# Interleaving two float32 tensors: the first x tile loaded as four half-height pieces from two DMA rings

## The chip, the cores and the metric

The kernel runs on one core of a Trainium2 chip. The metric is the device time in microseconds of one execution, of which the runs shown give the median. A span is what the profiler recorded of one execution, from the program's first instruction to its last.

## The reference

Two tensors of 32 x 256 x 1024 float32 are woven into one of twice the width: elements of x on the even places of the last dimension, elements of y on the odd ones. Nothing is calculated.

```python
batch, seq, dim = x.shape                 # 32, 256, 1024
result = np.zeros((batch, seq, dim * 2), dtype=np.float32)
result[..., 0::2] = x
result[..., 1::2] = y
```

x and y are 33.55 MB each and the result is 67.11 MB, so 134.22 MB pass between HBM and SBUF.

## The kernel before

Because weaving doesn't depend on where a row ends, the kernel treats each tensor as one flat run of numbers. It cuts x and y into n = 8 tiles of 128 partitions by W = 8192 numbers (4 MB each), and the result into 8 tiles of 128 by 2W. One partition's share of a tile is 32 KB, contiguous in HBM. There are two buffers for x (`xt`), two for y (`yt`) and two for the output (`ot`); an output buffer holds one half (h = 0 or 1) of an output tile, 128 x 8192 numbers or 4 MB, made from H = 4096 columns of x and the same columns of y.

Three engines do the work, each with a loop of its own over the tiles, and they meet only through semaphores:

- SyncE issues all loads on its own DMA ring. The first x tile is loaded in two column halves (L42, which counts on `xsem[0]`, and L43, which counts on `hsem`). Then follow, tile by tile, x (L50) and y (L53), each as one transfer. From the third tile on it first waits (`woven`, counted by the copies) until the copies have read the old contents of the buffer.
- VectorE makes two copies per half tile: x to the even places of `ot[h]` (L67) and y to the odd ones (L70). Ahead of the copy of x it waits for the x tile, and for the stores of that output buffer to be over (`osem`, and for the second tile `qsem`).
- ScalarE issues all stores on its own ring, one per half tile (L83), after the second copy of that half. The very first half tile's store is made in two parts: the first quarter of the columns (L77) and the rest (L81).

A DMA adds 16 to its semaphore when it is complete, which is why waits are for multiples of 16. At the end ScalarE clears the semaphores and SyncE waits for the last store (L91).

The program begins with a barrier of all engines (in the traces under L99 and L137, the lines of the call). `tile_interleave_kernel` moves transfers ahead of it after the program is built: for each entry in the list of L104 it takes that engine's first remaining DMA from the later blocks, requires that it has no wait, and inserts it into the first block ahead of that engine's drain, with which the engine enters the barrier. Before the change the list has SyncE twice, so the two halves of the first x tile (L42, L43) are issued ahead of the barrier. The y tile of L53 is then SyncE's first transfer behind it.

Of the kernel before, what the change touches and what calls it, by code (L numbers as in the profile page):

```python
# [3 lines left out]


def _interleave(nc, x, y, out):
    P = 128
    W = 8192
    H = W // 2  # L10

    total = 1
    for s in x.shape:
        total *= s
    n = total // (P * W)
    assert n * P * W == total

    def rows(ap, names, k):
        flat = ap.rearrange("b s d -> (b s d)")
        return flat[k * names : (k + 1) * names].rearrange("(p w) -> p w", p=P)  # L20

    fp32 = mybir.dt.float32
    xt = [nc.alloc_sbuf_tensor(f"xt{b}", [P, W], fp32).ap() for b in (0, 1)]
    yt = [nc.alloc_sbuf_tensor(f"yt{b}", [P, W], fp32).ap() for b in (0, 1)]
    ot = [nc.alloc_sbuf_tensor(f"ot{b}", [P, W], fp32).ap() for b in (0, 1)]

    xsem = [nc.alloc_semaphore(f"xsem{b}") for b in (0, 1)]
    hsem = nc.alloc_semaphore("hsem")
    qsem = nc.alloc_semaphore("qsem")
    ysem = [nc.alloc_semaphore(f"ysem{b}") for b in (0, 1)]  # L30
    woven = nc.alloc_semaphore("woven")
    osem = [nc.alloc_semaphore(f"osem{b}") for b in (0, 1)]


    cuts = [0, W // 4, W]
    parts = [slice(a, b) for a, b in zip(cuts, cuts[1:])]

    xs = [rows(x, P * W, k) for k in range(n)]
    ys = [rows(y, P * W, k) for k in range(n)]
    os_ = [rows(out, 2 * P * W, k) for k in range(n)]  # L40

    nc.sync.dma_start(out=xt[0][:, :H], in_=xs[0][:, :H]).then_inc(xsem[0], 16)  # L42
    nc.sync.dma_start(out=xt[0][:, H:], in_=xs[0][:, H:]).then_inc(hsem, 16)  # L43

    for k in range(n):
        b = k % 2
        if k >= 2:
            nc.sync.wait_ge(woven, 4 * (k - 2) + 3)
        if k:
            nc.sync.dma_start(out=xt[b], in_=xs[k]).then_inc(xsem[b], 16)  # L50
        if k >= 2:
            nc.sync.wait_ge(woven, 4 * (k - 2) + 4)
        nc.sync.dma_start(out=yt[b], in_=ys[k]).then_inc(ysem[b], 16)  # L53

    for k in range(n):
        b = k % 2
        for h in (0, 1):
            c = slice(h * H, (h + 1) * H)
            if h == 0:
                nc.vector.wait_ge(xsem[b], 16 * (k // 2 + 1))  # L60
            elif k == 0:
                nc.vector.wait_ge(hsem, 16)
            if k:
                nc.vector.wait_ge(osem[h], 16 * k)
            if (k, h) == (1, 0):
                nc.vector.wait_ge(qsem, 16)
            nc.vector.tensor_copy(out=ot[h][:, 0::2], in_=xt[b][:, c]).then_inc(woven, 1)  # L67
            if h == 0:
                nc.vector.wait_ge(ysem[b], 16 * (k // 2 + 1))
            nc.vector.tensor_copy(out=ot[h][:, 1::2], in_=yt[b][:, c]).then_inc(woven, 1)  # L70

    for k in range(n):
        for h in (0, 1):
            nc.scalar.wait_ge(woven, 4 * k + 2 * h + 2)
            if (k, h) == (0, 0):
                for c in parts[:-1]:
                    nc.scalar.dma_start(  # L77
                        out=os_[k][:, c], in_=ot[h][:, c]
                    ).then_inc(qsem, 16)
                c = parts[-1]  # L80
                nc.scalar.dma_start(out=os_[k][:, c], in_=ot[h][:, c]).then_inc(osem[h], 16)  # L81
                continue
            nc.scalar.dma_start(  # L83
                out=os_[k][:, h * W : (h + 1) * W], in_=ot[h]
            ).then_inc(osem[h], 16)

    nc.scalar.wait_ge(osem[0], 16 * n)
    used = sorted(s.num for s in [*xsem, hsem, qsem, *ysem, woven, osem[0]])
    assert used == list(range(used[0], used[-1] + 1)), used
    nc.scalar.sem_clear(range(used[0], used[-1] + 1))  # L90
    nc.sync.nop(nofuse=True).wait_op(osem[1], 16 * n, "sem-ge").then_inc(  # L91
        osem[1], -16 * n
    )


def kernel(tc, x, y, out):
    nc = tc.nc
    tc.close()
    tc.compile()  # L99

    _interleave(nc, x, y, out)

    blocks = nc.main_func.blocks
    for engine in (mybir.EngineType.SP, mybir.EngineType.SP):  # L104
        opening = blocks[0].instructions
        at, moved = next(
            (b, i)
            for b in blocks[1:]
            for i in b.instructions
            if i.engine == engine and i.opcode == "DMACopy"  # L110
        )
        assert not (moved.sync_info and moved.sync_info.on_wait)
        body = at.instructions
        body.remove(moved)
        gate = next(
            n
            for n, i in enumerate(opening)
            if i.engine == engine and i.opcode == "Drain"
        )
        opening.insert(gate, moved)  # L120
        at.instructions = body
        blocks[0].instructions = opening


# [1 line left out]
_INS = ['x', 'y']  # L126
_OUTS = [((32, 256, 2048), 'float32')]


# [23 lines left out]
```

## Time and profile before

| What | Value |
|---|---|
| Time, median of 3 runs | 314.18 us (314.18 to 314.37) |
| Span of the profiled execution | 312.9 us, 114 instructions (the page gives no other time of it) |
| VectorE | 72.0 us busy, 23%, 32 copies: L67 36.7 us, 2295 ns each; L70 36.6 us, 2288 ns each |
| GpSimd | 0.2 us, four memsets of the opening |
| TensorE, ScalarE | no busy time (ScalarE only issues DMAs) |
| DMA | 134.22 MB in 4896 packets, mean 429 GB/s |
| Idle time ahead of L67 | 213.8 us, of it 206.5 until stores are over, 7.3 until the first x is there |
| Idle time ahead of L70 | 12.3 us, once, until the first y is there |
| From issue to landing | store of 4 MB 34.1 us; y 41.5; x 24.3; first x halves 7.3 and 11.8 (medians) |

Idle time of an engine that isn't the bottleneck costs nothing. VectorE's 213.8 us are of this kind if the transfers run on during it. The time from issue to landing has the waiting behind earlier transfers in it, and is far above what a transfer's own bytes take.

### The profile page before, as it was taken

What the parts mean: (1) busy time and instruction counts of PE and PEld (TensorE: products, weight loads), DVE (VectorE), ACT (ScalarE), POOL (GpSimd) and SP (SyncE); (2) the same over time, 40 slices, a digit from 0 to 9 for tenths busy, and PEclk for the clock granted to TensorE, in tenths of its full rate; (3) what the DMA queues carried; (4) which work ended last, traced back from release to release, by engine and by line L of the source; (5) the groups of instructions that cost most, each with busy time, mean ns of one, the idle gap of its engine ahead of it and who ended that gap; (6) DMA issues with size and microseconds to landing.
All of it is one profiled execution on the core that took longest, in us unless ns stands there. A gap on an engine that the chain in (4) does not pass through costs nothing.

```text
span 312.9 us, 114 instructions
## 1 busy us (share of the span) xinstructions
DVE 72.0 (23%) x32; POOL 0.2 (0%) x4
## 2 busy tenths in 40 slices
DVE  0216000501305023050220503205032050415410
POOL 0000000000000000000000000000000000000000
DMA  8999999999999999999999999999999999999998
GB/s 337 467 402 436 436 402 419 452 457 415 427 444 411 461 402 469 402 469 402 469 402 465 406 440 432 423 448 402 469 402 469 402 469 402 469 402 448 423 423 381
DMA packets 4896, 134.22 MB, mean 429 GB/s; under 512 B 544, under 2 KB 544, under 8 KB 544
## 3 DMA queue, kind: packets, MB, share of 16 engines
q1 hardware_dynamic: 2448, 67.11, 50.1%
q10 hardware_dynamic: 2448, 67.11, 49.7%
HBM read 67.11 MB, written 67.11 MB: 429 GB/s over the span
## 4 chain that ended last, share of the span: by engine, by line
DMA 82%; DVE 12%; issue 0%
DMA out_dram<-ot 76%; DMA yt<-in_y_dram 6%; DVE ot L70 6%; DVE ot L67 6%
## 5 line engine op out<-in xcount | busy, mean ns | idle before, releaser
L67 DVE COPY ot<-xt 128x4096 f32<-128x4096 f32 x16 | 36.7, 2295 | 213.8 <-DMA out_dram<-ot 206.5
L70 DVE COPY ot<-yt 128x4096 f32<-128x4096 f32 x16 | 36.6, 2288 | 12.3 <-DMA yt<-in_y_dram 12.3
L137 POOL MEMSET const-bfloat16-1.0<- 128x1 bf16 x1 | 0.1, 103 | 0.0
L137 POOL MEMSET const-uint8-127<- 128x1 uint8 x1 | 0.1, 102 | 0.0
L137 POOL MEMSET const-float32-0.0<- 128x1 f32 x1 | 0.1, 100 | 0.2 <-issue 0.2
L137 POOL MEMSET const-float32-1.0<- 128x1 f32 x1 | 0.1, 99 | 0.0
## 6 DMA issues: line engine op xcount, KB each, us to landing
out_dram<-ot ACTq DMA_DIRECT2D x15, 4096.0 KB, 34.1
yt<-in_y_dram SPq DMA_DIRECT2D x8, 4096.0 KB, 41.5
xt<-in_x_dram SPq DMA_DIRECT2D x7, 4096.0 KB, 24.3
xt<-in_x_dram SPq DMA_DIRECT2D x2, 2048.0 KB, 9.5
out_dram<-ot ACTq DMA_DIRECT2D x1, 3072.0 KB, 32.8
out_dram<-ot ACTq DMA_DIRECT2D x1, 1024.0 KB, 16.3
```

The costliest lines, as they stand in the source:

```text
L67: nc.vector.tensor_copy(out=ot[h][:, 0::2], in_=xt[b][:, c]).then_inc(woven, 1)
L70: nc.vector.tensor_copy(out=ot[h][:, 1::2], in_=yt[b][:, c]).then_inc(woven, 1)
L137: nc = _bacc.Bacc("TRN2", target_bir_lowering=False, num_devices=1)
```

## The change

The first x tile is loaded by four transfers instead of two. Each moves 64 partitions (rows of the tile) by 4096 columns, 1 MB. The lower 64 rows are issued by SyncE, the upper 64 by ScalarE, each with the left columns first. One of the four counts on `xsem[0]` and the other three on `hsem`, which so reaches 48. The first copy of x now waits for both, that is for the whole tile; before, it waited for the left half, and the second half's copy for the right one. The list of transfers that are moved ahead of the barrier gets two entries for ScalarE beside SyncE's two, and ScalarE's first two transfers are the two upper pieces.

```diff
-    nc.sync.dma_start(out=xt[0][:, :H], in_=xs[0][:, :H]).then_inc(xsem[0], 16)
-    nc.sync.dma_start(out=xt[0][:, H:], in_=xs[0][:, H:]).then_inc(hsem, 16)
+    lower, upper = slice(0, P // 2), slice(P // 2, P)
+    opening = [
+        (nc.sync, lower, slice(0, H), xsem[0]),
+        (nc.sync, lower, slice(H, W), hsem),
+        (nc.scalar, upper, slice(0, H), hsem),
+        (nc.scalar, upper, slice(H, W), hsem),
+    ]
+    for engine, p, c, sem in opening:
+        engine.dma_start(out=xt[0][p, c], in_=xs[0][p, c]).then_inc(sem, 16)
...
             if h == 0:
                 nc.vector.wait_ge(xsem[b], 16 * (k // 2 + 1))
-            elif k == 0:
-                nc.vector.wait_ge(hsem, 16)
+                if k == 0:
+                    nc.vector.wait_ge(hsem, 48)
...
-    for engine in (mybir.EngineType.SP, mybir.EngineType.SP):
+    for engine in (
+        mybir.EngineType.SP,
+        mybir.EngineType.SP,
+        mybir.EngineType.Activation,
+        mybir.EngineType.Activation,
+    ):
```

## The prediction

> **What bounds the kernel now.** I read the busy line and the slices of the page first, then its DMA queues, then the chain of waits, then the first 30 us instruction by instruction, and last the stretches of the opening.
>
> ```profile
> DVE 72.0 (23%) x32; POOL 0.2 (0%) x4
> DMA  8999999999999999999999999999999999999998
> q1 hardware_dynamic: 2448, 67.11, 50.1%
> q10 hardware_dynamic: 2448, 67.11, 49.7%
> HBM read 67.11 MB, written 67.11 MB: 429 GB/s over the span
> DMA 82%; DVE 12%; issue 0%
> ```
>
> VectorE works 23% of the span. The 16 DMA engines are at nine tenths or more in every slice but the first and the last, and the two rings together (q1 is SyncE's, all loads; q10 is ScalarE's, all stores) take 50.1 + 49.7 = 99.8% of their time. The kernel is as long as its bytes: 134.22 MB over 312.9 us. So a microsecond in which the engines move less than they can is not regained later, and a wait of VectorE counts only if it leaves both rings empty. The DMA work of the last tile ends the span in the same way, so I carry every loss or gain of the opening to the end at its full size.
>
> ```profile
> 0.00 0.37 SPq L42 DMA_DIRECT2D xt<-in_x_dram  x1
> 0.42 0.42 SPq L43 DMA_DIRECT2D xt<-in_x_dram  x1
> 1.90 0.33 SPq L53 DMA_DIRECT2D yt<-in_y_dram  x1
> 7.33 2.30 DVE L67 COPY ot<-xt 128x4096 f32<-128x4096 f32 x1 [7.33 <-DMA xt<-in_x_dram]
> 21.91 2.29 DVE L70 COPY ot<-yt 128x4096 f32<-128x4096 f32 x1 [12.28 <-DMA yt<-in_y_dram]
> 24.12 2.29 DVE L67 COPY ot<-xt 128x4096 f32<-128x4096 f32 x1
> 24.24 0.38 ACTq L77 DMA_DIRECT2D out_dram<-ot  x1
> ```
>
> SyncE issues the two column halves of the first x tile at 0.00 and 0.42; the first y tile, behind the barrier, at 1.90. The first copy runs from 7.33 to 9.63 and VectorE then stands 12.28 us until y has landed. What of the opening matters is therefore y at 21.91, and what gives that time is two 4 MB tiles in a row on one ring. The first half of x had landed at 7.3 us and the second, issued at 0.42, 11.8 us later, at 12.2: one 2 MB half takes 12.2 - 7.3 = 4.86 us (7.31 and 12.17 in the trace), and y's 4 MB 21.89 - 12.17 = 9.72 us, twice that. Both are 432 GB/s.
>
> ```profile
> 0.00:1.90 1.90, 0.00 (x0) 0.20 (x4) 1.00 0.60 129
> 1.90:12.00 10.10, 2.30 (x1) 0.00 (x0) 1.00 1.04 443
> 12.00:22.00 10.00, 0.09 (x1) 0.00 (x0) 1.00 0.97 419
> 22.00:47.00 25.00, 6.61 (x3) 0.00 (x0) 1.00 1.00 419
> ```
>
> The columns are stretch, length, VectorE, GpSimd, clock, DMA share and GB/s (a packet's bytes count where it ends, so a share can pass 1). Only the stretch up to 1.90 is slack. The packet records have the first x packet at 0.99 us, a microsecond behind its issue, and an engine's first packet of 16 KB takes 1.15 to 1.48 us where the median one takes 0.61. From 1.9 us on there is nothing to win.
>
> **The change part by part.** *Issues.* SyncE still issues two transfers ahead of the barrier, each half as high. Their 0.37 + 0.42 us I leave as they are. ScalarE issues two as well. In the trace it stands at its first drain 0.14 us after SyncE's first issue, and its two issues would take what SyncE's took, so it is done near 0.14 + 0.37 + 0.05 + 0.42 = 0.98 against SyncE's 0.84. The barrier, which now waits for SyncE, would wait for ScalarE, 0.14 us longer, and y's issue goes from 1.90 to about 2.04. That is free as long as the SyncE ring holds x packets: its 2 MB last until at least 1.0 + 4.86 = 5.9 us even if it had all engines to itself. Without this cover it would cost 0.14 us. Behind ScalarE's issues stand its first wait for a copy (24.24 now) and nothing earlier; GpSimd's four memsets are over at 0.43.
>
> *The wait.* The first copy now needs all four pieces (hsem at 48 beside xsem at 16). With x in at 12.17 as now, it runs to 14.5, and y lands at 21.89: 7.4 us of cover. Queued behind it on VectorE are the y copy and then the store of L77, and both wait for y anyway. It costs nothing while x comes less than 7.4 us late relative to y. Since y is behind x's lower half on the same ring, and alternates with the upper one, y would be late too, so I charge nothing here.
>
> *The start.* The same engines begin at the same time behind the same first issue. A second ring could at most fill the wait inside an engine's first packet, 1.3 - 0.61 = 0.7 us. That is the bound of a gain; I take 0, since the second packet of an engine follows its first directly now, so the ring isn't short of descriptors.
>
> *The transfer of 64 rows.* This is the one large unknown: every transfer in this trace is 128 rows high. All 128 rows at once move at 432 GB/s; a piece is now 64 x 16 KB, 1 MB. Lower bound: the time goes by bytes alone. The packets speak for it (8, 16, 24 and 32 KB take 0.31, 0.61, 0.91 and 1.21 us), each piece takes 2.43 us, four of them 9.72, cost 0. Upper bound: a piece of half the height takes as long as one of full height, because what it goes through is halved with the partitions, and the two rings don't make up for it: 4 x 4.86 - 9.72 = +9.72 us. What decides between them is how much of the time both halves are under way together on every engine. Two rows bear on it. Where both rings have work they alternate packet by packet: the 1 MB store of L77 lands 16.3 us behind its issue, though its bytes are worth 2.43, because each of its 8 KB packets stands behind a 32 KB load packet (0.31 + 1.21 us, eight times, is 12.2). And a ring that comes second comes late: that store is issued at 24.24 and its first packet starts at 28.64 in the packet records, 4.4 us later where the first x packet needed 1.0. So I take the lower first piece to run without its partner, at the full-height price, 4.86 - 2.43 = **+2.43 us**, and the other three, alternating with the opposite half or with full-height y rows, at the price by bytes. I choose this value and don't read it; it lies nearer to the lower bound because the packet rows do.
>
> [...]
>
> **Sum.** The span of 312.86 us and 1.32 us around it are the median of 314.18 (the page has no time of its own beside the span; the runs shown lie between 314.18 and 314.37). 0 for issues, wait and start, +2.43 for the lone piece: span 315.29, time **316.6 us**. Its own range is 314.8 to 319.1: from the least that counts as slower to both lower pieces running alone (2 x 2.43 = 4.86).
>
> **Rivals.** *The halves never help each other (323.9 us, or some way towards it).* Each engine alternates a lower and an upper row, and all engines do so in step; then at any time only one half of the partitions takes data, and all four pieces cost the full-height 4.86. 314.18 + 9.72 = 323.9; with engines partly out of step, 319.1 upwards. For it: rings alternate strictly, and ScalarE's ring starts within 0.14 us of SyncE's on all engines. Against it: the engines' first packets start anywhere from 0.99 to 1.3 us and beyond, half a packet's time apart, and this spread would persist. [...]
>
> *By bytes alone (314.2 us, same).* The place is the engine itself: if 26.8 GB/s per engine (16 KB in 0.611 us) is the limit, whatever the height, or if 64 rows go to other engines than the other 64, nothing moves. It decides as soon as the lower pieces' packets take 0.61 us from the start; price 0 to 0.14 us. For it: the packet times by bytes, the same for loads and stores. Against it: all of them belong to transfers over all partitions. Here too belongs that the edit doesn't take hold: the reordering moves the first two copies that ScalarE has, which are the upper pieces; it could fail only in order, and would then add the late-ring price of the forecast instead.
>
> *A better start (313.5 us, faster).* Two rings fill the 0.7 us inside the first packets: 314.18 - 0.7. For it: the DMA share is 0.60 up to 1.90 us. Against it: that is a latency, present in each ring.
>
> **Chances and range.** Forecast 0.40, in step 0.20, by bytes 0.30, better start 0.10. About 0.2% (0.63 us) is what a measurement of this kernel can tell from no change. Faster by more than that is the better start alone, 0.10; within it, by bytes, 0.30; slower, the forecast and the halves in step, 0.60. The range is 313.6 to 321.5: it leaves out most of the better start and the upper half of the in-step case, 319.1 to 323.9, about 0.2 together.
>
> **What would show it.** In the changed trace: the x pieces' landings and y's. Forecast: x all in near 14.6 us, y near 24.3, the y copy of L70 and everything behind it 2.4 us later, and after 25 us the same stretches as now. In step: y near 31, and GB/s in the first slices near half. By bytes: x at 12.2 and y at 21.9 as now. Better start: both 0.7 earlier. The first copy should start with x's last landing and end ahead of y; if VectorE's copy comes after y has landed, I have mispriced the wait. If y is early or late by one amount and the end by another, my rule that the opening is carried whole to the end is wrong.

## The result, and the profile after

The changed kernel takes 323.3 us (322.95 to 323.92, 5 runs) against 314.29 us (314.18 to 314.37, 5 runs): a ratio of 1.029, 95% interval 1.0278 to 1.0302. It is 9.0 us slower. The profiled execution, with a span of 322.6 us, is the longest of the five (322.6 + 1.3 = 323.9); against the span of before it lost 9.7 us.

From the page of the changed kernel, the lines that answer to those shown of before, with the slices of what was moved:

```profile
DVE 72.0 (22%) x32; POOL 0.2 (0%) x4
DMA  8999999999999999999999999999999999999998
GB/s 197 228 291 394 434 444 423 445 425 431 451 419 431 451 418 431 451 419 427 455 419 427 455 419 427 455 418 427 455 414 431 455 414 431 455 414 431 455 414 366
q10 hardware_dynamic: 2608, 69.21, 51.1%
q1 hardware_dynamic: 2320, 65.01, 48.5%
```

The DMA engines look as busy as before, at nine tenths in every slice but the ends, and their rings still fill 51.1 + 48.5 = 99.6% of the span. But the first three slices (8 us each) moved 197, 228 and 291 GB/s, where the others, but for the last, run at 394 to 455. The busy share doesn't show the loss, since a slow packet counts as busy; the bytes do. 2.1 MB, the upper half of one x tile, have gone from q1 to q10.

The first 35 us of the changed kernel, instruction by instruction (left out are four memsets, two later load issues, and what follows the first store's first issue):

```profile
0.00 1.18 SPq L50 DMA_DIRECT2D xt<-in_x_dram  x2
0.12 1.33 ACTq L50 DMA_DIRECT2D xt<-in_x_dram  x2
...
2.77 0.34 SPq L60 DMA_DIRECT2D yt<-in_y_dram  x1
...
26.02 2.29 DVE L74 COPY ot<-xt 128x4096 f32<-128x4096 f32 x1 [26.02 <-DMA xt<-in_x_dram]
32.03 2.30 DVE L77 COPY ot<-yt 128x4096 f32<-128x4096 f32 x1 [3.72 <-DMA yt<-in_y_dram]
34.24 2.29 DVE L74 COPY ot<-xt 128x4096 f32<-128x4096 f32 x1
34.36 0.35 ACTq L84 DMA_DIRECT2D out_dram<-ot  x1
```

The whole x tile is in at 25.9 us instead of 12.2, and y at 32.0 instead of 21.9: 10.1 us late. From there the order and the spacing are those of before. The first store goes out 2.33 us behind the y copy's start, as before, and the end is 9.7 us late; 0.4 us come back on the way (the second part of the first store lands 32.4 us behind its issue, 32.8 before).

Three stretches of the opening, of the kernel before and then of the changed one (length, VectorE, GpSimd, clock, DMA share, GB/s):

```profile
2.00:6.00 4.00, 0.00 (x0) 0.00 (x0) 1.00 0.94 397
6.00:12.00 6.00, 2.30 (x1) 0.00 (x0) 1.00 1.12 478
12.00:18.00 6.00, 0.00 (x0) 0.00 (x0) 1.00 1.01 437
```

```profile
2.00:6.00 4.00, 0.00 (x0) 0.00 (x0) 1.00 0.99 217
6.00:12.00 6.00, 0.00 (x0) 0.00 (x0) 1.00 0.99 229
12.00:18.00 6.00, 0.00 (x0) 0.00 (x0) 1.00 1.09 257
```

Same busy share, half the bytes. In the packet records a 16 KB packet of x takes about 1.28 us in the first stretch and 1.09 to 1.25 in the next two, where it took 0.61. The four pieces land at 8.94 and 18.02 (lower), 15.65 and 25.92 us (upper). Three of them count on `hsem` together; whose landing is whose was read from the two rings' packets, which end at 13.61 us for the first upper piece and at 15.96 for the second lower one. The last upper piece has y's rows of full height beside it and is slow all the same: its last two packets per engine take 1.22 us, and the three y packets that alternate with them 1.72, 1.65 and 1.60 (medians) instead of 1.21.

### The profile page after: what moved, and what is told of

Same layout as the page of the kernel before. It is cut to its first block, busy times and chain, and to the rows that moved or that the text cites. A ratio compares the mean times of both kernels' runs of the same rounds, so it can differ in the third digit from the quotient of the medians.

```text
span 322.6 us, 117 instructions
## 1 busy us (share of the span) xinstructions
DVE 72.0 (22%) x32; POOL 0.2 (0%) x4
## 3 DMA queue, kind: packets, MB, share of 16 engines
q10 hardware_dynamic: 2608, 69.21, 51.1%
q1 hardware_dynamic: 2320, 65.01, 48.5%
## 4 chain that ended last, share of the span: by engine, by line
DMA 83%; DVE 12%; issue 0%
DMA out_dram<-ot 74%; DMA yt<-in_y_dram 9%; DVE ot L77 6%; DVE ot L74 6%
## 5 line engine op out<-in xcount | busy, mean ns | idle before, releaser
L77 DVE COPY ot<-yt 128x4096 f32<-128x4096 f32 x16 | 36.6, 2289 | 3.7 <-DMA yt<-in_y_dram 3.7
## 6 DMA issues: line engine op xcount, KB each, us to landing
out_dram<-ot ACTq DMA_DIRECT2D x1, 3072.0 KB, 32.4
```

## The experiments

Three theories at first. A: the lower and the upper 64 rows go into SBUF by separate ways, and the engines write to one half at a time. B: two rings that load at once get in each other's way. C: any transfer of 64 rows is slow. Where no time of before stands beside a result, it is 314.22 us in the first four runs and 314.27 in the second four. e1 to e3 and e5 to e7 are edits of the changed kernel, the others of the kernel before. In the code, `...` stands for lines left out, among them the list of transfers that are moved ahead of the barrier, which goes with each edit.

**e1: two rings, rows not split.**

```diff
     opening = [
-        (nc.sync, lower, slice(0, H), xsem[0]),
-        (nc.sync, lower, slice(H, W), hsem),
-        (nc.scalar, upper, slice(0, H), hsem),
-        (nc.scalar, upper, slice(H, W), hsem),
+        (nc.sync, every, slice(0, H), xsem[0]),
+        (nc.scalar, every, slice(H, W), hsem),
     ]
...
-                    nc.vector.wait_ge(hsem, 48)
+                    nc.vector.wait_ge(hsem, 16)
...
```

> Two rings kept, rows not split: SyncE loads the left columns of all 128 rows, ScalarE the right ones. Theory A (lower and upper rows go through different halves of the way into SBUF, and the engines alternate between the halves in step): every packet back at 0.61 us, y in at 21.9 to 22.3, time within 0.5 us of before. Theory B (two rings loading at once get in each other's way, whatever the rows): packets at 1.2 us, y near 32, time near 323. Theory C (any transfer 64 rows high is slow): as A here.

Measured: 314.28 us, ratio 1.0001 (0.9991 to 1.001), y in at 22.1. B falls: two rings loading at once, and the wait for the whole tile, cost nothing.

**e2: rows split, one ring.** All four pieces are issued by SyncE.

```diff
-        (nc.scalar, upper, slice(0, H), hsem),
-        (nc.scalar, upper, slice(H, W), hsem),
+        (nc.sync, upper, slice(0, H), hsem),
+        (nc.sync, upper, slice(H, W), hsem),
...
```

> Rows split, one ring: all four half-height pieces from SyncE, both lower ones first. Theory A: each piece at the price of a full-height one, 4 x 4.86 us, y near 31.6, time 323 to 324, so that ScalarE's ring neither helps nor harms. Theory B: no second ring, no cost, time near 314.3. Theory C: as A.

Measured: 324.27 us, ratio 1.0319 (1.0303 to 1.0334). The pieces land at 7.89, 12.83, 17.89 and 22.90 us, 4.94 to 5.06 apart, where 1 MB at the old rate is worth 2.43. The same stretch as above:

```profile
6.00:12.00 6.00, 0.00 (x0) 0.00 (x0) 1.00 1.03 216
```

The loss needs no second ring.

**e3: another 64 rows first.**

```diff
-    lower, upper = slice(0, P // 2), slice(P // 2, P)
+    middle = slice(P // 4, 3 * P // 4)
     opening = [
-        (nc.sync, lower, slice(0, H), xsem[0]),
-        (nc.sync, lower, slice(H, W), hsem),
-        (nc.scalar, upper, slice(0, H), hsem),
-        (nc.scalar, upper, slice(H, W), hsem),
+        (nc.sync, middle, slice(0, H), xsem[0]),
+        (nc.sync, middle, slice(H, W), hsem),
+        (nc.sync, slice(0, P // 4), slice(0, W), hsem),
+        (nc.sync, slice(3 * P // 4, P), slice(0, W), hsem),
     ]
...
```

> One ring; first rows 32 to 95 in two column halves of 1 MB each, 64 rows high as the changed kernel's pieces but half from the lower and half from the upper 64; then rows 0 to 31 and rows 96 to 127 at full width, 1 MB each. Theory A: the middle pieces' packets take 0.61 us and both are in near 7.3 us, the two outer ones cost 4.86 us each where 2.43 is their share by bytes, y near 26.8, time near 319.1 (+4.9). Theory C: the middle pieces take 4.86 us each as well, y near 31.6, time 323 to 324. [...]

Measured: 319.27 us, ratio 1.0159 (1.0144 to 1.0174). The stretch of the middle rows, the one of the outer rows, and one of y, from the trace of e3:

```profile
2.00:6.00 4.00, 0.00 (x0) 0.00 (x0) 1.00 0.90 385
8.00:15.00 7.00, 0.00 (x0) 0.00 (x0) 1.00 1.07 225
18.00:26.00 8.00, 2.29 (x1) 0.00 (x0) 1.00 1.06 459
```

Sixty-four rows run at 385 GB/s if they are rows 32 to 95, packets at 0.61 us; rows 0 to 31 and 96 to 127 run at 225. C falls: not how many rows, but which. The middle pieces were in at 8.2 us, not 7.3: their last packet ended at 7.23 instead of 6.97 us, behind a first one at 1.39 instead of 0.99, and the landing came 0.92 us after it instead of 0.34. What made it so was not tried.

**e4: the wait alone**, in the kernel before.

```diff
-            elif k == 0:
-                nc.vector.wait_ge(hsem, 16)
+                if k == 0:
+                    nc.vector.wait_ge(hsem, 16)
```

> The kernel before with only the wait changed: the first copy waits for the whole x tile. All theories: first copy from 12.2 instead of 7.3 us, y copy unchanged at 21.9, time within 0.3 us of before. If this costs, the wait has a part in the loss.

Measured: 314.21 us, ratio 0.9999 (0.9989 to 1.0008); first copy at 12.48, y copy at 22.12. The wait is free.

**e5: half the dose.**

```diff
+        (nc.sync, slice(0, P), slice(0, H), xsem[0]),
         (nc.sync, lower, slice(H, W), hsem),
-        (nc.scalar, upper, slice(0, H), hsem),
         (nc.scalar, upper, slice(H, W), hsem),
     ]
...
-                    nc.vector.wait_ge(hsem, 48)
+                    nc.vector.wait_ge(hsem, 32)
...
```

> Half the dose: the left columns at full height from SyncE, the right columns as a lower piece from SyncE and an upper one from ScalarE. Theory A (1 MB of 64 lower or 64 upper rows costs 4.86 us instead of 2.43, however the two are interleaved): two such pieces, +4.86, time near 319.1. If a fixed price of the second ring or of the row cut were at work, the loss would stay near 9.

Measured: 320.06 us (319.29 to 320.23), ratio 1.0178 (1.0163 to 1.0193); span 318.0, 5.1 over before, y in at 27.5. The loss goes roughly by the bytes that move in half-height pieces: +5.1 us of span for 2 MB, +9.7 for 4 MB. The profiled execution is the shortest of its four here and was the longest above; by the medians it is +5.8 and +9.0. A fixed price near 9 is ruled out either way.

**e6: even and odd rows.** The changed kernel with `lower, upper = slice(0, P, 2), slice(1, P, 2)`.

> The changed kernel with another cut: SyncE loads the even rows, ScalarE the odd ones, four pieces of 64 rows by 4096 columns, so every piece has rows of both halves. Theory A1 (only the cut between rows 0 to 63 and 64 to 127 matters): packets at 0.61 us, time near 314.5. Theory A2 (a finer grouping matters: an engine now takes four rows two apart, and engines that are in step may again meet at the same place while others stand empty): packets near 1.2 us, time up to 323. [...]

Measured: 314.5 us, ratio 1.0008 (0.9999 to 1.0018), packets at 0.61 us:

```profile
6.00:12.00 6.00, 0.00 (x0) 0.00 (x0) 1.00 1.02 437
```

Four pieces of 64 rows, two rings, the same wait, the same four issues: no loss that can be told from none. What is left is which 64 rows a piece has. The run also prices the issues: the first packet starts at 1.33 us instead of 0.99, and y lands 0.23 us later than before.

**e7: eight engines one packet behind.**

```diff
+    eight = slice(0, P // 4, 4)
+    nc.sync.dma_start(out=ot[1][eight, :H], in_=xs[0][eight, :H]).then_inc(hsem, 16)
...
-                    nc.vector.wait_ge(hsem, 48)
+                    nc.vector.wait_ge(hsem, 64)
...
```

> The changed kernel, with eight extra rows loaded ahead of it by SyncE, one packet of 16 KB each, to a place that is overwritten later (128 KB more to move); if they go to eight of the engines alone, these are one packet behind the other eight from then on. Theory A (the loss is there because all engines write to the same half at the same time): out of step, each engine pair uses both halves at once while the rings alternate; only the pieces that run alone pay, 1 MB or so; loss +2 to +4, time 316.5 to 318.5. If the packets stay at 1.2 us and the time near 323.5, being in step is not what costs, or the engines fall back into step.

Measured: 324.12 us, ratio 1.0312 (1.0297 to 1.0328). In the packet records, eight packets of each ring are under way at 7, 8 and 14 us, and both rings have some at every full microsecond from 7 to 15 us; still all take 1.1 to 1.3 us. So "all engines on one half at once" alone doesn't explain the limit; the halves of theory A are too coarse. The next runs measure the transfers by themselves (e8, which follows m1, turns to stores).

**m1: loads alone.** Thirteen sets of loads, ahead of the kernel before, each issued when the last has landed. m1 to m4 are one execution each; sets that come back in another of these runs differ by at most 0.25 us. One set in the code:

```python
nc.sync.dma_start(out=ot[0][32:96, :], in_=xs[1][0:64, :]).then_inc(tsem, 16)
done += 16
nc.sync.wait_ge(tsem, done)
```

> Ahead of the kernel before, thirteen loads run alone, each issued when the last has landed (the kernel's own time grows by their sum and means nothing). Rows of 32 KB go to places that are overwritten later. From the rows so far a 2 MB load of 64 rows lands 6.5 to 7.5 us behind its issue at full rate and 11 to 12 at half. All 128 rows: 11 to 12 us (4 MB). Rows 0 to 63 and 64 to 127: half rate; rows 32 to 95 and the even rows: full. What no run has told apart: is it where a row lies in HBM or where it goes in SBUF? If SBUF, HBM rows 0 to 63 to partitions 32 to 95 run at full rate and HBM rows 32 to 95 to partitions 0 to 63 at half; if HBM, the other way round. Is it the half or a finer group? Four loads of 16 rows, eight rows apart (2 MB): by halves full rate, 7 to 8 us; by groups of four neighbouring rows, two engines on each, half, 11 to 12. Four loads of 16 rows four apart in the lower half: half rate by either. Eight rows (8 engines, 1 MB in four loads): four apart in the lower half, 7 to 8 us by either, the engines' own rate; eight apart in the lower half, the same by halves, up to 12 by groups. Last, the two halves of the rows from two rings at once, 4 MB: near 21 if the rings don't help each other, 11 to 12 if they do.

From the trace of m1, the first issue of each set (start, time of the issue). A set lasts until the next one starts:

```profile
1.38 0.38 SPq L44 DMA_DIRECT2D ot<-in_x_dram  x1
13.61 0.55 SPq L47 DMA_DIRECT2D ot<-in_x_dram  x1
26.36 0.47 SPq L50 DMA_DIRECT2D ot<-in_x_dram  x1
39.16 0.55 SPq L53 DMA_DIRECT2D ot<-in_x_dram  x1
46.79 0.52 SPq L56 DMA_DIRECT2D ot<-in_x_dram  x1
54.47 0.49 SPq L59 DMA_DIRECT2D ot<-in_x_dram  x1
67.05 0.51 SPq L62 DMA_DIRECT2D ot<-in_x_dram  x1
74.69 0.52 SPq L65 DMA_DIRECT2D ot<-in_x_dram  x1
...
87.43 0.49 SPq L71 DMA_DIRECT2D ot<-in_x_dram  x1
...
99.84 0.74 SPq L77 DMA_DIRECT2D ot<-in_x_dram  x1
...
107.84 0.58 SPq L83 DMA_DIRECT2D ot<-in_x_dram  x1
...
120.51 0.56 SPq L89 DMA_DIRECT2D ot<-in_x_dram  x1
...
132.81 0.50 SPq L96 DMA_DIRECT2D ot<-in_x_dram  x1
132.81 0.53 ACTq L97 DMA_DIRECT2D ot<-in_x_dram  x1
154.81 0.35 SPq L102 DMA_DIRECT2D xt<-in_x_dram  x1
```

| Line | Rows in SBUF | MB | us (difference of starts) |
|---|---|---|---|
| L44 | 0 to 127 | 4 | 12.2 |
| L47, L50 | 0 to 63; 64 to 127 | 2 | 12.8; 12.8 |
| L53 | 32 to 95 | 2 | 7.6 |
| L56 | 32 to 95, from HBM rows 0 to 63 | 2 | 7.7 |
| L59 | 0 to 63, from HBM rows 32 to 95 | 2 | 12.6 |
| L62 | even rows | 2 | 7.6 |
| L65 | 16 rows, eight apart (0, 8, ... 120), four times | 2 | 12.7 |
| L71 | 16 rows, four apart (0, 4, ... 60), four times | 2 | 12.4 |
| L77 | 8 rows, four apart (0, 4, ... 28), four times | 1 | 8.0 |
| L83 | 8 rows, eight apart (0, 8, ... 56), four times | 1 | 12.7 |
| L89 | 8 rows, sixteen apart (0, 16, ... 112), four times | 1 | 12.3 |
| L96, L97 | 0 to 63 and 64 to 127, two rings | 4 | 22.0 |

L56 against L59, 7.7 against 12.6 us, puts the limit at the place in SBUF: with other HBM rows the times moved by 0.2 us at most (L53 7.6, L47 12.8). L65 spreads its rows evenly over both halves and is slow at 12.7 us, so halves are not the unit. L77 against L83: 1 MB takes 8.0 us on rows 0, 4, ... 28, and 12.7 on rows 0, 8, ... 56. One reading, an inference from these times: rows of one half that lie 32 apart share a place, and two engines at one place take about 2.5 us each for 32 KB, where one alone takes 1.21. The 2.5 is an estimate from L47 and L53, four packets per engine each: 1.21 + (12.8 - 7.6) / 4. Every slow set has such a partner for each of its rows (L83 rows 0 and 32, 8 and 40 and so on), and L53, L56 and L77, at 7.6, 7.7 and 8.0 us, have no such pair; no set had such a pair alone. All 128 rows (L44) and the even rows (L62) have the pairs as well and are fast at 12.2 us for 4 MB and 7.6 for 2 MB; there the reading needs that the engines of a pair seldom be at it together, in L47 that they be. Which engine has which row, the trace doesn't say. That groups of four neighbouring rows go together, as was expected, no set shows.

**e8: stores.** In the kernel before, the very last store is issued in two parts, rows 0 to 63 by ScalarE and 64 to 127 by SyncE.

```diff
+            if (k, h) == (n - 1, 1):
+                low, up = slice(0, P // 2), slice(P // 2, P)
+                nc.scalar.dma_start(
+                    out=os_[k][low, W:], in_=ot[h][low]
+                ).then_inc(osem[h], 16)
+                nc.sync.wait_ge(woven, 4 * n)
+                nc.sync.dma_start(
+                    out=os_[k][up, W:], in_=ot[h][up]
+                ).then_inc(qsem, 16)
+                continue
...
+    nc.scalar.wait_ge(qsem, 32)
```

> The kernel before, with the very last store (4 MB) cut into its lower 64 rows from ScalarE and its upper 64 from SyncE; loads as before. If reading SBUF has the same limit by halves as writing it, and the two rings run in step: the last store takes up to twice its 9.7 us, time up to 323.9. If the two rings' halves are out of step here, or reads are not limited: near 314.3. The run tells whether the loss belongs to loads alone.

Measured: 317.95 us, ratio 1.0112 (1.0096 to 1.0129). It lies between. Its packets of 32 KB take 1.21 to 2.42 us, and the records show when (each engine's first, at 1.21, apart). At 305 and 307 us all sixteen packets under way are of one ring, and they take 1.3 to 2.2 us. At 309 and 310 both rings have five or more under way, and most take 1.21 to 1.5. At 314 only ScalarE's are left, and they take 1.96 to 2.42. So opposite halves can help each other; why they do so here and not in the changed kernel is open.

**m2: who shares, and stores alone.** Nine sets; those of interest, in short (rows as first:end:step):

```python
# set 2: sync rows r:32:4, scalar rows 64+r:96:4, r = 0..3
# set 3: sync rows 64+r:96:4 (eight rows), r = 0..3, then rows 0:64
# set 4: the same eight, then 0:32:2, 1:32:2, 32:64:2, 33:64:2
# sets 6 to 9: stores of rows 0:128, 0:64, 32:96, and 0:64 with 64:128
```

> Ahead of the kernel before, nine sets of transfers run one after the other, each set alone (the kernel's own time means nothing). [...] Set 2: eight engines alone, eight lower rows four apart from SyncE and eight upper ones from ScalarE, four times, 2 MB. No place is shared. If an engine alternates between halves freely, 11.5 to 12.5 us from issue to the last landing at 1.21 us per packet; if alternating itself costs, up to 20. Set 3: eight engines get four packets of upper rows each, then all sixteen the lower 64 rows (3 MB). If the two engines that share a place are one of the eight and one of the others, being out of step helps: 12 to 13.5 us; if both belong to the same eight, it can't: 16.5 to 18. [...] Set 5: sixteen rows four apart from row 32, no place shared: 7 to 8 us. Then stores of what set 1 loaded (to a part of the result that is overwritten later): all 128 rows 11.5 us; rows 0 to 63 near 7.5 if reading SBUF has no such limit and near 12 if it has; rows 32 to 95 near 7.5; both halves from two rings at once, 4 MB, 11.5 or up to 21. The run before with its last store cut by rows lost 3.7 us, which lies between.

Set 2 took 12.6 us at 1.21 us a packet: an engine that alternates between halves pays nothing. Sets 3 and 4 both took 19 us, longer than either value expected for set 3. Set 5 took 8.4 us with its four issues. The stores, in the trace of m2 (the next event, the first load of the kernel, is at 122.52):

```profile
72.67 0.35 ACTq L85 DMA_DIRECT2D out_dram<-ot  x1
83.80 0.56 ACTq L89 DMA_DIRECT2D out_dram<-ot  x1
95.71 0.58 ACTq L93 DMA_DIRECT2D out_dram<-ot  x1
102.37 0.51 ACTq L97 DMA_DIRECT2D out_dram<-ot  x1
102.43 0.52 SPq L98 DMA_DIRECT2D out_dram<-ot  x1
```

All rows 11.1 us (4 MB); rows 0 to 63 11.9 us for half of it; rows 32 to 95 6.7; both halves on two rings 20.1. By these sets, reading SBUF has the same price. Finer groups of rows, and SBUF rows apart from HBM rows, were not tried with stores.

**m3b: the same eight?** Sets of the same kind: eight busy engines, then sixteen rows.

> Six more sets of loads, each alone, ahead of the kernel before (its own time means nothing). In the last run eight engines were kept busy first with four packets each (upper rows, one place each), and the lower 64 rows behind them still ran at 2.5 us per packet. Either the engines that share a place belong to the same eight, or keeping them apart in time doesn't help. Set 2: sixteen lower rows four apart, four times, alone: 11 to 12 us as before. Set 3: the same behind the eight busy engines: the places are shared by the j-th and the (j+8)-th row of each transfer. If the eight busy engines are those of the first eight rows and time apart helps, the others run at 1.21 us and the set is through in 12.5 to 14.5 us; if time apart doesn't help, or the eight are spread, 17 to 19. Set 4: busy with lower rows, then sixteen rows from 32, four apart (first eight lower, last eight upper, no two on one place): 12.5 to 14.5 if the eight are the first eight, since the others then write upper rows only; set 5, busy with upper rows, then the same sixteen: longer than set 4 if the eight are the first eight, equal if they are spread. Set 6 repeats the last run's set 4, 19.

Measured, as differences of starts: set 2 12.5, set 3 17.5, set 4 13.3, set 5 14.4, set 6 18.9 us. Set 4 is shorter than set 5, so the eight are those of a transfer's first eight rows. The packets say so too: the engines that join the busy ones take 1.34 to 2.11 us for their first packet and mostly 1.21 for the next in set 4, but 2.0 to 2.4 and then 2.1 to 2.3 in set 5. Set 3 was expected at 12.5 to 14.5 or at 17 to 19, and the lower bound was mine to see: its 2 MB are rows 0 to 63, which no set moved alone in under 12.4 us (L71 of m1), and at e2's 216 GB/s they take 9.7 us from the first of them, which started 5.5 us into the set (31.69 us, in a set from 26.16). So by this estimate at least 15.2 us were due, and keeping engines apart in time can't pay there. The same bound holds for sets 3 and 4 of m2 (first lower packets 5.4 and 5.0 us into the set), so their 19 us don't tell who shares. Being apart can pay only where the other half's rows are at hand, which the last run tries.

**m4: out of step, with both halves at hand.** Lower rows from SyncE and upper ones from ScalarE, as sixteen rows four apart; 0 to 3 packets ahead on eight engines (sets 2 to 5). Sets 6 and 7: pieces of 64 rows, with none and one.

```python
# set 3
nc.sync.dma_start(out=ot[1][64:96:4, :], ...)            # eight rows ahead
nc.sync.dma_start(out=ot[0][r:64:4, :], ...)             # r = 0..3
nc.scalar.dma_start(out=ot[0][64 + r : 128 : 4, :], ...) # r = 0..3
```

> Seven sets of loads, each alone, ahead of the kernel before (its own time means nothing). Sets 2 to 5: 4 MB on two rings as in the changed kernel, lower rows from SyncE and upper from ScalarE, but in transfers of sixteen rows four apart, so that rows j and j+8 of a transfer share a place; the first eight engines are given 0, 1, 2 or 3 packets of 32 KB ahead, from SyncE. Set 6: as the changed kernel, pieces of 64 rows, nothing ahead; set 7: the same with one packet ahead. If the two rings fail to help each other only because engines that share a place stay in step, sets 2 and 6 take 20 to 22 us, and at least one of sets 3 to 5, where they are out of step, 12 to 16; set 7 stays with 6 if in a piece of 64 rows the sharers are both among the first eight. If sets 3 to 5 stay at 20 us or more, being in step is not the reason, and it stays open.

Measured: sets 2 to 5 21.9, 18.2, 22.6 and 22.3 us; set 6 22.2, set 7 25.9. From the trace of m4, a stretch of sets 2, 3, 6 and 7 each:

```profile
16.00:34.00 18.00, 0.00 (x0) 0.00 (x0) 1.00 0.94 208
42.00:48.00 6.00, 0.00 (x0) 0.00 (x0) 1.00 1.06 399
102.00:118.00 16.00, 0.00 (x0) 0.00 (x0) 1.00 1.08 229
124.00:144.00 20.00, 0.00 (x0) 0.00 (x0) 1.00 0.99 197
```

In set 3, between 42 and 48 us, eight packets of each ring, so of each half, are under way; those that start from 43.5 us on take 1.29 to 1.44 us, and the stretch moves 399 GB/s. So two rings with opposite halves ran near the full rate here, at 399 GB/s against 208 in set 2; by the reading of m1, because the engines that share a place were on different rings' packets. The total was still 18.2 and not 12 to 16: each engine's first packet takes 1.90 to 2.69 us and its second 2.55, and from 48.9 us on only lower rows are left, at 1.5 to 2.45 us. Two and three packets ahead (sets 4 and 5) brought nothing. In set 7 the same shift brings nothing. The reading that fits, with e7, is that in a piece of 64 rows the engines that share a place are both among the first eight, and are shifted together; no run names the engine of a row, so this stays an inference.

Two pieces of 64 rows on two rings (set 6) took 22.2 us, against 12.4 for one transfer of the same 4 MB (set 1), as if one half had followed the other; set 3's 399 GB/s shows that it isn't so in every case.

## Why the prediction was wrong

*What bounds the kernel, and that the opening is carried to the end:* right. y 10.1 us late, the end 9.7 us.

*The wait:* right, e4 and e1 show no cost; VectorE still stood 3.7 us for y behind the late first copy.

*The start:* right that two rings don't win the 0.7 us of a first packet (e1, 314.28 us; first packet at 1.01). The 1.15 to 1.48 us of first packets hold for twelve of the sixteen engines; the four that start last, from 1.61 us on, take 0.61 to 1.00.

*The issues:* the mechanism was right and the size was off. I left the issues of half-height pieces at 0.37 and 0.42 us. They take 0.55 and 0.58 on SyncE and 0.54 and 0.75 on ScalarE, the drain behind them 0.37 to 0.40 instead of 0.13, and y's issue goes to 2.77, not 2.04. That was covered, as I said, by the x packets. The first packet at 1.35 instead of 0.99 us has no cover; by e6 it is worth 0.2 us in y's landing; the median there is 0.2 longer too, which its interval doesn't tell from none.

*The transfer of 64 rows:* here the step failed that let "the other three, alternating with the opposite half or with full-height y rows" run at the price by bytes. The lone first piece came out as priced: a piece alone costs 4.9 to 5.1 us (e2), twice 2.43, and ScalarE's ring did come late, its first packet at 5.63 us against SyncE's 1.35, though issued 0.12 us behind. But the other three cost about twice their bytes as well: alternating with the opposite half took a packet from 1.28 us only to 1.09 to 1.25, where 0.61 was assumed, and beside y's rows of full height it was no better, where y's packets lost time too. 9.72 for four pieces and 0.2 to 0.36 for the first packet make 9.9 to 10.1, and y was 10.12 late. The upper bound of the unknown was the answer. (The range's 319.1 for two lone pieces is 314.18 + 4.86 = 319.04; nothing hangs on it.)

I leaned to the lower bound because packet times go by bytes in the trace of before. Those rows had no bearing on the question: all were of transfers over 128 rows, and in m1 4 MB of these took 12.2 us (L44), 2 MB of rows 0 to 63 12.8 (L47). The rival in which the halves never help each other, at 0.20, is what happened; its 323.9 is the profiled execution's time (the median is 323.3), and the range's 321.5 cut it off. Its reason, that the engines alternate in step, holds in part. In the changed kernel all sixteen packets under way are of one ring at 7.0 and 7.5 us, but eight are of each at 6.5, 10 and 11 us, and the packets then take 1.09 to 1.29 us all the same. m4's set 3 shows that being in step matters (18.2 us against 21.9 in set 2), and e7 that not any step apart helps (324.12 us). Why the halves that are under way together don't help each other in pieces of 64 rows stays open, but for the inference at the end of m4.

## What to carry to other kernels

Cut a transfer between HBM and SBUF by columns (e1, 314.28 us), or by rows so that a piece is like rows 32 to 95 or every second row (m1, 7.6 us for 2 MB); a piece of rows 0 to 63 took 12.8 us, and a second ring with rows 64 to 127 didn't mend it (22.0 us for 4 MB). In a kernel that is bound by DMA, read GB/s beside the busy share: slow packets count as busy (from 2 to 6 us a share of 0.99 at 217 GB/s here, 0.94 at 397 before). A bound from rows that were all taken under one condition says nothing of the other condition; then the far end deserves the larger chance.

## What the runs showed of the hardware that was not expected

- Stores pay the same price by the SBUF rows that they read: rows 0 to 63 11.9 us, rows 32 to 95 6.7 us for 2 MB.
- A ring that is issued 0.12 us behind another got its first packet 4.3 us behind it (5.63 against 1.35 us): every engine first took the other ring's four packets. The number isn't fixed: in e1 it was two (2.84 against 1.01 us).
- The issue of a transfer of 64 rows takes longer than that of 128 rows in the same place (SyncE's first two: 0.55 and 0.58 us against 0.37 and 0.42). Over these runs it is 0.47 to 0.75 against 0.33 to 0.53 us, and 0.56 to 0.81 for 8 rows, once 1.51 (m2).
